# Modulation sums paired with fixed VectorE operations, and the one-row Fourier split ahead of the others

## The chip, the cores and the metric

The kernel runs on one core of a Trainium2 chip. The metric is the device time of one execution in microseconds (us); lower is better.

## What is computed

One layer of a diffusion block on 1024 latent tokens of 1024 features, with 256 context tokens. The reference, cut to what matters here:

```python
mod = cond @ w_mod[l] + b_mod[l]                  # cond = silu(c): one row of 1024
sh1, sc1, g1, sh2, sc2, g2 = jnp.split(mod[:, None, :], N_MOD, axis=-1)
hx = modulate(rmsnorm(x, norm1_g[l]), sh1, sc1)
u_f, u_x, u_g = split(hx @ w_in)                  # 512 features each
y_f = fft2(u_f by groups, norm="ortho").real      # Fourier half, 4 groups of 128
y_r = bidir_rglru(u_x, ...)                       # conv, gates, scans in two directions
x_mix = concat([y_f, y_r * gelu(u_g)]) @ w_out
x = x + g1 * x_mix
hx2 = modulate(rmsnorm(x, norm2_g[l]), sh2, sc2)
x = x + g2 * expert_choice_ffn(hx2, ...)          # 16 experts, top-k routed
return rmsnorm(x, final_g)
```

`sh1` and `sc1` are wanted at once, `g1`, `sh2`, `sc2` and `g2` only after the output projection. Each of these four rows is a sum over 1024 condition values times rows of `w_mod`.

## The kernel before

The program has five parts in time. A prologue (to about 88 us) sums `sh1` and `sc1` on TensorE, norms and transposes the tokens, and projects the first two `u_x` column tiles. `phase_c` (about 88 to 255 us) has the rest of the combined input projection and all that hangs on it. `phase_f` (to about 345 us) has the Fourier matmuls `pq`, the output projection `mx`, the residual and the router. Then a stream of 16 experts (`gu`, `y`) runs to the end, bound by TensorE.

Matmuls are done at full fp32 precision by three products: each operand is split into a high and a low half. ScalarE writes the high half (L227), VectorE the low half as a difference (L228). In names, `wh`/`wl` are the halves of a projection weight (`wr` raw), `gh`/`gl` those of a gate weight, `abh`/`abl` and `xh`/`xl` those of the first Fourier step's result (`ab`, and `abx`, which is a single row). `split` gives one ScalarE and one VectorE instruction; here all splits of `get` and `fb_split` are made at a raised priority.

`phase_c` runs over four tiles t of 128 recurrent features. For each: a projection `ux`, a causal convolution on VectorE (`conv`, L658, result `xc`), gate matmuls `g`, `lru_front` (sigmoids, `r` and `g`; `g*xc` on VectorE, L697 to L700; exponentials to `a` on ScalarE, L707), `lru_back` (a square root on ScalarE, L805, then for each direction the three VectorE operations of `lru_scan`: L713, L714 and the scan L716, and the add of both directions, L813), and `gelu` (projection `ug` of column tile 8+t, a gelu on ScalarE, L821, and a product on VectorE, L822). Beside it run the four Fourier column tiles: `fourier_a` (projection `uf`, VectorE writes sum and difference `U`), then `fb_dft` (`ab`, `abx`), `fb_split`, `fb_trig` (`pq`, a single buffer in PSUM) and `fb_evac` (VectorE operations on `T` and `yf`, L947 to L956, which empty `pq`). `get(ct)` loads and splits the weights of column tile ct: 0 to 3 are `uf`, 4 to 7 `ux`, 8 to 11 `ug`.

The four late modulation rows are summed on VectorE by `mod_acc(r, h)`, called eight times (four rows r, two halves h of 512 columns). One call goes over eight blocks of 128 condition values in four pairs. A pair is one load of 512 KB (`mraw`, two buffers, issued by GpSimd) and two VectorE operations of 128x512 that add it into `macc`; the first of a sum is a TENSOR_SCALAR (L837), the other seven are SCALAR_TENSOR_TENSOR (L839). In all there are 32 loads and 64 operations; the eight sums are stored by GpSimd and read in `phase_f`.

The order of each engine's instructions is set by a tile scheduler when the program is built, by priority (earlier code first, raised for those under `high_priority`) and by when its own model finds operands ready. Instructions handed to `pin` keep their written order among themselves on one engine and are passed through the scheduler as a fixed list; the rest stay free to move. `mod_acc` is not pinned before.

Of the kernel before, what the change touches and what calls it, by code (L numbers as in the profile page):

```python
# [9 lines left out]
F32 = mybir.dt.float32  # L10
# [4 lines left out]
ALU = mybir.AluOpType  # L15

D = 1024
N = 1024
NCTX = 256
L = N + NCTX  # L20
KD = 8
# [140 lines left out]
class Kern:  # L162
# [486 lines left out]
    def conv(self, t):  # L649
        nc = self.nc  # L650
        u = self.u.pop(t)
        xc = self.c5(f"xc{t}", tag="xc")
        col = lambda i: self.cols[:, COL["cw"] + 4 * i + t:COL["cw"] + 4 * i + t + 1]
        cb = self.cols[:, COL["cb"] + t:COL["cb"] + t + 1]
        for o, n, q in ((0, N, NCTX), (N, NCTX, 0)):
            nc.scalar.activation(xc[:, q:q + n], u[:, o:o + n], AF.Identity, scale=col(1), bias=cb)
            for i, a, b in ((0, 1, n), (2, 0, n - 1), (3, 0, n - 2)):
                nc.vector.scalar_tensor_tensor(xc[:, q + a:q + b], u[:, o + a + i - 1:o + b + i - 1], col(i),  # L658
                                               xc[:, q + a:q + b], op0=ALU.mult, op1=ALU.add)
        self.xc[t] = xc  # L660

    def xsplit(self, t):
# [47 lines left out]

    def lru_scan(self, d, r, g, a):
        V = self.nc.vector
        V.scalar_tensor_tensor(r, a, 1.0, r, op0=ALU.add, op1=ALU.mult)  # L713
        V.tensor_tensor(r, r, g, op=ALU.mult)  # L714
        s = slice(None) if d == 0 else slice(None, None, -1)
        V.tensor_tensor_scan(g[:, s], a[:, s], r[:, s], 0.0, op0=ALU.mult, op1=ALU.add)  # L716

    def phase_c(self, stop=None):
        nc = self.nc
        self.xc, self.xs, self.graw, self.gw = {}, {}, {}, {}  # L720
        self.ysp = self.dram.tile([7, 128, N], F32, name="ysp")
        self.yl = {}
        self.accd = self.dram.tile([4, 2, 128, 512], F32, name="accd")
        st = {}
        self.load_gate(0)
        self.conv(0)
        self.xsplit(0)
        self.load_trig()
        self.ux(2)
        self.gate_w(0)  # L730
        self.get(7)
        st[0] = self.lru_front(0)
        self.load_gate(1)
        self.conv(1)
        self.xsplit(1)
        self.ux(3)
        self.get(0)
        self.gate_w(1)
        self.lru_back(0, *st[0])
        self.fourier_a(0)  # L740
        self.mod_acc(0, 0)
        self.conv(2)
        self.get(8)
        self.load_gate(2)
        st[1] = self.lru_front(1)
        self.mod_acc(0, 1)
        self.xsplit(2)
        self.gelu(0)
        self.mod_acc(1, 0)
        self.gate_w(2)  # L750
        self.get(1)
        self.lru_back(1, *st[1])
        self.conv(3)
        self.fourier_a(1)
        self.mod_acc(1, 1)
        self.get(9)
        self.load_gate(3)
        st[2] = self.lru_front(2)
        self.mod_acc(2, 0)
        self.xsplit(3)  # L760
        self.gelu(1)
        self.mod_acc(2, 1)
        self.gate_w(3)
        self.get(2)
        self.lru_back(2, *st[2])
        self.fourier_a(2)
        self.mod_acc(3, 0)
        self.get(3)
        st[3] = self.lru_front(3)
        self.fourier_a(3)  # L770
        self.get(10)
        self.lru_back(3, *st[3])
        self.gelu(2)
        self.get(11)
        self.fd = {}
        self.fb_dft(0)
        self.fb_split(0)
        self.gelu(3)
        self.mod_acc(3, 1)
        if stop == "e":  # L780
            self.fd = {}
            for g in range(CT):
                self.fb_dft(g)
                self.fb_split(g)
                self.fb_trig(g)
                self.fb_evac(g)
# [21 lines left out]
    def lru_back(self, t, st, a):  # L808
        nc = self.nc
        for d in range(2):  # L810
            self.lru_scan(d, *st[d], a[d])
        g0, g1 = st[0][1], st[1][1]
        nc.vector.tensor_tensor(g0[:, NCTX:], g0[:, NCTX:], g1[:, 0:N], op=ALU.add)  # L813
        self.yl[t] = g0[:, NCTX:]

    def gelu(self, t):
        nc = self.nc
        p = self.p2(f"ug{t}")
        self.proj(p, 8 + t)
        gg = self.pr.tile([128, N], F32, tag="gg", name=f"gg{t}", bufs=1)  # L820
        nc.scalar.activation(gg, p, AF.Gelu_apprx_tanh)  # L821
        nc.vector.tensor_tensor(gg, gg, self.yl.pop(t), op=ALU.mult)  # L822
        self.dump(f"yr{t}", gg)
        nc.sync.dma_start(self.ysp[3 + t], gg)

    def mod_acc(self, r, h):
        nc, a = self.nc, self.a
        m, s = (2, 4, 3, 5)[r], slice(512 * h, 512 * h + 512)
        acc = self.pr.tile([128, 512], F32, tag="ht", name=f"macc{m}{h}", bufs=2)
        for kp in range(KD // 2):  # L830
            w = self.pro.tile([128, 2, 512], F32, tag="mraw", name=f"mraw{m}{h}{kp}", bufs=2)
            nc.gpsimd.dma_start(w, a["wmod"][m, 2 * kp:2 * kp + 2, :, s].rearrange("k p c -> p k c"))
            for i in range(2):
                k = 2 * kp + i
                c = self.cond[:, k:k + 1]
                if k == 0:
                    nc.vector.tensor_scalar(acc, w[:, i], c, None, op0=ALU.mult)  # L837
                else:
                    nc.vector.scalar_tensor_tensor(acc, w[:, i], c, acc, op0=ALU.mult, op1=ALU.add)  # L839
        nc.gpsimd.dma_start(self.accd[r, h], acc)  # L840

    def mod_row(self, r, acc, b, ones, p):
        nc = self.nc
# [32 lines left out]
    def fourier_a(self, g):  # L876
        nc = self.nc
        V = nc.vector
        p = self.p2(f"uf{g}")
        self.proj(p, g)  # L880
        U = self.c4(f"U{g}", (128, 2, 512))
        uT = self.pr.tile([128, 512], F32, tag="uT", name=f"uT{g}", bufs=1)
        nc.scalar.activation(uT, p[:, 1023:511:-1], AF.Copy)
        rev = uT[:, 0:511]
        V.tensor_tensor(U[:, 0, 1:], p[:, 1:512], rev, op=ALU.add)
        V.tensor_tensor(U[:, 1, 1:], p[:, 1:512], rev, op=ALU.subtract)
# [19 lines left out]
    def fb_split(self, g):  # L906
        p, px = self.fd[g]
        hi, lo = self.c4(f"abh{g}", (128, 8, 128), F32R), self.c4(f"abl{g}", (128, 8, 128), F32R)
        xh = self.pr.tile([1, 128], F32R, tag="xh", name=f"xh{g}", bufs=1)
        xl = self.pr.tile([1, 128], F32R, tag="xl", name=f"xl{g}", bufs=1)  # L910
        with self.tc.high_priority(offset=self.HP):
            for s in range(2):
                self.split(p[:, 512 * s:512 * s + 512].rearrange("p (a b) -> p a b", b=128),
                           hi[:, 4 * s:4 * s + 4], lo[:, 4 * s:4 * s + 4])
            self.split(px[0:1, 0:128], xh, xl)
        self.fd[g] = hi, lo, xh, xl

    def fb_trig(self, g):
# [910 lines left out]
```

## Time and profile before

| what | us |
|---|---|
| time before, median of 3 runs | 1969.02 (1968.03 to 1969.90) |
| the profiled execution, its own time | 1968.55 |
| its span from first to last instruction | 1966.7 |
| TensorE busy in the span | 1883.7 (96%) |
| VectorE busy | 1749.7 (89%) |
| ScalarE busy | 1357.4 (69%) |
| the 56 SCALAR_TENSOR_TENSOR of `macc` | 41.8 |

All rows below are of one profiled execution. TensorE's matmul stream is PE, its weight loads PEld; VectorE is DVE, ScalarE ACT, GpSimd POOL. A group row gives the busy time and mean duration; an arrow `<-` in square brackets names what ended the idle time ahead of an instruction.

### The profile page before, as it was taken

Reading aid. Unit: us, or ns where it says so; the run is one execution under the profiler, and the core shown is the slowest. Engines: PE = TensorE matmul, PEld = TensorE weight load, DVE = VectorE, ACT = ScalarE, POOL = GpSimd, SP = SyncE. Lnnn points to the kernel's source line nnn. Section 1 sums busy time; section 2 is a strip of 40 time slices with the busy share of each in tenths; the row PEclk is TensorE's granted clock in tenths of the full one; section 3 lists DMA queues with packets and bytes.
Section 4 is the critical chain, followed back from the end, with each engine's and each line's share of the span. In section 5 each row is a group of like instructions: output and inputs, shape, how many; then the busy total and the mean of one; then the engine's idle time right before and its main releaser. Section 6 shows DMA issues by size and latency. Waiting matters only on the chain.

```text
span 1966.7 us, 23514 instructions
## 1 busy us (share of the span) xinstructions
PE 1883.7 (96%) x8944; PEld 1530.9 (78%) x8944; DVE 1749.7 (89%) x1626; ACT 1357.4 (69%) x1094; POOL 126.6 (6%) x126
## 2 busy tenths in 40 slices
PE   7989879969999999999999999999999999999996
PEld 2777767857788888888888888888888888888884
DVE  7889787789999989899999999998989898989987
ACT  6568643346677777777777777777777777777775
POOL 2311100220000000000000000000000000000000
PEclk9999989979999999999999999999999999999998
DMA  8443554578999999999999999999999999999994
GB/s 333 126 148 123 193 174 150 200 279 332 352 352 388 383 376 390 370 395 371 391 362 395 359 409 370 387 364 397 372 384 380 391 379 373 390 383 390 371 391 172
DMA packets 113952, 651.27 MB, mean 331 GB/s; under 512 B 12743, under 2 KB 20472, under 8 KB 46254
## 3 DMA queue, kind: packets, MB, share of 16 engines
q1 hardware_dynamic: 100718, 602.55, 79.6%
q0 software_dynamic: 10816, 38.82, 7.0%
q10 hardware_dynamic: 2304, 8.39, 1.1%
q8 instruction: 70, 1.15, 0.2%
q14 instruction: 44, 0.36, 0.0%
HBM read 622.98 MB, written 26.74 MB: 330 GB/s over the span
## 4 chain that ended last, share of the span: by engine, by line
PE 79%; DVE 8%; DMA 6%; issue 5%; ACT 1%; POOL 0%; SPq 0%; POOLq 0%; DVEq 0%; ACTq 0%
PE gu L611 46%; PE y L611 23%; PE mx L611 4%; DMA mraw<-in_wmod_dram 3%; DVE lo L228 3%; PE ht L1620 2%; DMA wm<-in_wmod_dram 1%; DVE macc L839 1%; PE xt L1492 1%; DMA trr<-in_trig_dram 1%; PE hp L1185 1%; PE pq L611 1%; ACT hi L227 1%; DVE g L716 0%; DVE r L714 0%
## 5 line engine op out<-in xcount | busy, mean ns | idle before, releaser
L228 DVE TENSOR_TENSOR lo<-raw,hi 128x2048 fp32r<-128x2048 f32 x525 | 1196.9, 2295 | 120.6 <-ACT hi L227 119.7
L227 ACT ACTIVATE hi<-raw 128x2048 fp32r<-128x2048 f32 x525 | 1007.0, 1918 | 303.2 <-PE gu L611 204.4
L611 PE MATMUL gu<-hi,xgh 128*128 128x512 f32 x1408 | 556.2, 395 | 0.0
L611 PE MATMUL gu<-lo,xgh 128*128 128x512 f32 x1408 | 548.7, 390 | 1.4 <-DVE lo L228 1.4
L611 PE MATMUL gu<-hi,xgl 128*128 128x512 f32 x1408 | 548.9, 390 | 0.0
L611 PEld LDWEIGHTS gu<-hi,xgl 128*128 128x128 f32 x1408 | 264.4, 188 | 56.4 <-DVE xgl L228 0.2
L611 PEld LDWEIGHTS gu<-lo,xgh 128*128 128x128 f32 x1408 | 264.8, 188 | 55.7 <-DVE lo L228 1.8
L611 PEld LDWEIGHTS gu<-hi,xgh 128*128 128x128 f32 x1408 | 264.6, 188 | 52.7 <-issue 0.2
L611 PE MATMUL y<-hi,hh 128*128 128x512 f32 x704 | 282.0, 401 | 0.0
L611 PE MATMUL y<-hi,hl 128*128 128x512 f32 x704 | 275.9, 392 | 1.3 <-DVE hl L228 1.3
L611 PE MATMUL y<-lo,hh 128*128 128x512 f32 x704 | 274.8, 390 | 0.0
L611 PEld LDWEIGHTS y<-hi,hl 128*128 128x128 f32 x704 | 132.4, 188 | 30.4 <-DVE hl L228 1.8
L611 PEld LDWEIGHTS y<-lo,hh 128*128 128x128 f32 x704 | 132.9, 189 | 25.9 <-issue 0.2
L611 PEld LDWEIGHTS y<-hi,hh 128*128 128x128 f32 x704 | 132.7, 189 | 25.3 <-issue 0.2
L1613 ACT ACTIVATE hid<-gu 128x512 f32<-128x512 f32 x96 | 54.0, 563 | 82.4 <-PE gu L611 82.4
L1630 POOL DMA_INDIRECT accx<-ys,idx x15 | 23.9, 1590 | 1002.8 <-DVE ys L1629 929.7
L228 DVE TENSOR_TENSOR hl<-ht,hh 128x512 fp32r<-128x512 f32 x96 | 61.3, 638 | 0.0
L1614 DVE TENSOR_TENSOR hid<-hid,gu 128x512 f32<-128x512 f32 x96 | 61.0, 635 | 0.0
L839 DVE SCALAR_TENSOR_TENSOR macc<-mraw,cond,macc 128x512 f32<-128x512 f32 x56 | 41.8, 747 | 20.4 <-DMA mraw<-in_wmod_dram 19.5
L1620 PE MATMUL ht<-k_ident,hid 128*128 128x128 f32 x352 | 54.2, 272 | 3.0 <-DVE hid L1614 3.0
L1620 PEld LDWEIGHTS ht<-k_ident,hid 128*128 128x128 f32 x352 | 43.8, 140 | 16.5 <-DVE hid L1614 4.5
L227 ACT ACTIVATE hh<-ht 128x512 fp32r<-128x512 f32 x96 | 52.0, 541 | 1.5 <-PE ht L1620 1.5
(430 smaller groups left out, 1791.4 us busy)
## 6 DMA issues: line engine op xcount, KB each, us to landing
raw<-in_wg_dram SPq DMA_DIRECT2D x160, 1024.0 KB, 7.1
raw<-in_wu_dram SPq DMA_DIRECT2D x160, 1024.0 KB, 7.5
raw<-in_wd_dram SPq DMA_DIRECT2D x160, 1024.0 KB, 7.6
raw<-in_wt_dram SPq DMA_DIRECT2D x32, 1024.0 KB, 7.8
mraw<-in_wmod_dram POOLq DMA_DIRECT2D x32, 512.0 KB, 4.7
raw<-in_wdt_dram SPq DMA_DIRECT2D x16, 1024.0 KB, 6.9
wm<-in_wmod_dram SPq DMA_DIRECT2D x16, 512.0 KB, 9.8
wr<-in_win_dram SPq DMA_DIRECT2D x24, 256.0 KB, 3.6
```

Of the source, the lines that this page charges most:

```text
L227: i = self.nc.scalar.activation(hi, src, AF.Copy)
L228: j = (eng or self.nc.vector).tensor_tensor(lo, src, hi, op=ALU.subtract)
L611: i = nc.tensor.matmul(out, l, r, start=st, stop=sp)
L839: nc.vector.scalar_tensor_tensor(acc, w[:, i], c, acc, op0=ALU.mult, op1=ALU.add)
L1185: self.pin(nc.tensor.matmul(q[:, 1024:1024 + E], hT[:, k], wr[:, k], start=k == 0, stop=k == KD - 1))
L1492: nc.tensor.transpose(p[:, 128 * i:128 * i + 128], xg[:, 128 * k:128 * k + 128], self.ident)
L1613: nc.scalar.activation(hid[:, 0:w], p[:, 0, 0:w], AF.Silu)
L1614: nc.vector.tensor_tensor(hid[:, 0:w], hid[:, 0:w], up, op=ALU.mult)
L1620: self.nc.tensor.transpose(q[:, c:c + 128], hid[:, c:c + 128], self.ident)
L1630: self.nc.gpsimd.indirect_dma_start(out=self.accx, out_offset=bass.IndirectOffsetOnAxis(ap=idx[:, :1], axis=0), in_=ys, in_offset=None, co ...
```

## The change

The eight calls of `mod_acc` are gone. In their place a generator, `mod_gen`, goes through the 32 pairs in order. It issues the load of one pair ahead, and pins loads, sums and stores. `tick(instruction, cost)` stands behind VectorE operations of the convolution, the scans, the add, the gelu product and `fourier_a`, each with a cost in us written in the code, and advances the generator by one pair for each 1.7 us of cost (`STEP`). The operations given to `tick` aren't pinned. Counting starts ahead of the first `lru_back`; pairs that are left are written at the end of `phase_c`. In `fb_split` the one-row split stands first and at doubled priority.

```diff
@@ conv
-                nc.vector.scalar_tensor_tensor(xc[:, q + a:q + b], ...)
+                self.tick(nc.vector.scalar_tensor_tensor(xc[:, q + a:q + b], ...),
+                          1.3 if n == N else 0.5)
@@ lru_scan
-        V.scalar_tensor_tensor(r, a, 1.0, r, op0=ALU.add, op1=ALU.mult)
-        V.tensor_tensor(r, r, g, op=ALU.mult)
+        self.tick(V.scalar_tensor_tensor(r, a, 1.0, r, op0=ALU.add, op1=ALU.mult), 1.5)
+        self.tick(V.tensor_tensor(r, r, g, op=ALU.mult), 1.5)
...
+        self.tick(V.tensor_tensor_scan(g[:, s], a[:, s], r[:, s], 0.0, op0=ALU.mult, op1=ALU.add), 2.8)
@@ phase_c
+        self.mg, self.cost = self.mod_gen(), None
...
         self.gate_w(1)
+        self.cost = 0.0
         self.lru_back(0, *st[0])
         self.fourier_a(0)
-        self.mod_acc(0, 0)
         self.conv(2)
...
-        self.mod_acc(3, 1)
+        for _ in self.mg:
+            pass
@@ lru_back: the add, cost 1.2; gelu: the product, cost 1.2; fourier_a: both U operations, 0.7 each
@@ in place of mod_acc
+    STEP = 1.7
+    def tick(self, i, cost):
+        if self.cost is None:
+            return
+        self.cost += cost
+        while self.cost >= self.STEP:
+            self.cost -= self.STEP
+            next(self.mg, None)
+    def mod_gen(self):
+        nc, a = self.nc, self.a
+        todo = [(r, h, kp) for r in range(4) for h in range(2) for kp in range(KD // 2)]
+        w, acc = {}, {}
+        def load(n):
+            if n < len(todo):
...
+                self.pin(nc.gpsimd.dma_start(w[n], ...))
+        load(0)
+        for n, (r, h, kp) in enumerate(todo):
+            load(n + 1)
...
+                if k == 0:
+                    self.pin(nc.vector.tensor_scalar(acc, w[n][:, i], c, None, op0=ALU.mult))
+                else:
+                    self.pin(nc.vector.scalar_tensor_tensor(acc, w[n][:, i], c, acc, op0=ALU.mult, op1=ALU.add))
+            del w[n]
+            if kp == KD // 2 - 1:
+                self.pin(nc.gpsimd.dma_start(self.accd[r, h], acc))
+            yield
@@ fb_split
         with self.tc.high_priority(offset=self.HP):
+            with self.tc.high_priority(offset=self.HP):
+                self.split(px[0:1, 0:128], xh, xl)
             for s in range(2):
                 self.split(p[:, 512 * s:512 * s + 512].rearrange("p (a b) -> p a b", b=128),
                            hi[:, 4 * s:4 * s + 4], lo[:, 4 * s:4 * s + 4])
-            self.split(px[0:1, 0:128], xh, xl)
```

**First order excerpt.** VectorE at the first pair of scans (`lru_scan` of tile 0, about 127 to 142 us in the trace of before). A number behind a name tells buffers of one tag apart. Before:

```order
L839 SCALAR_TENSOR_TENSOR macc_1369<-mraw_1382,cond,macc_1369 128x512 x2
L837 TENSOR_SCALAR macc_1475<-mraw_1476,cond 128x512
L839 SCALAR_TENSOR_TENSOR macc_1475<-mraw_1476,cond,macc_1475 128x512
L713 SCALAR_TENSOR_TENSOR r_983<-a_1014,r_983 128x1280
L713 SCALAR_TENSOR_TENSOR r_1008<-a_1017,r_1008 128x1280
L228 TENSOR_TENSOR gl_1128<-gr_1022,gh_1127 128x512
L714 TENSOR_TENSOR r_983<-r_983,g_984 128x1280
L714 TENSOR_TENSOR r_1008<-r_1008,g_1009 128x1280
L716 SCALAR_TENSOR_TENSOR g_984<-a_1014,r_983 128x1280
L716 SCALAR_TENSOR_TENSOR g_1009<-a_1017,r_1008 128x1280
L228 TENSOR_TENSOR wl_0_1226<-wr_0_1221,wh_0_1225 128x512
```

And with the change; the lines of the file are shifted, so that L714, L715, L717 and L810 are what L713, L714, L716 and L813 were, and L854 and L856 what L837 and L839 were:

```order
L717 SCALAR_TENSOR_TENSOR g_984<-a_1014,r_983 128x1280
L856 SCALAR_TENSOR_TENSOR macc_1137<-mraw_1133,cond,macc_1137 128x512
L715 TENSOR_TENSOR r_1008<-r_1008,g_1009 128x1280
L856 SCALAR_TENSOR_TENSOR macc_1137<-mraw_1135,cond,macc_1137 128x512
L717 SCALAR_TENSOR_TENSOR g_1009<-a_1017,r_1008 128x1280
L856 SCALAR_TENSOR_TENSOR macc_1137<-mraw_1135,cond,macc_1137 128x512
L810 TENSOR_TENSOR g_984<-g_984,g_1009 128x1024
L856 SCALAR_TENSOR_TENSOR macc_1137<-mraw_1141,cond,macc_1137 128x512
L228 TENSOR_TENSOR wl_0_1259<-wr_0_1254,wh_0_1258 128x512
L856 SCALAR_TENSOR_TENSOR macc_1137<-mraw_1141,cond,macc_1137 128x512
L228 TENSOR_TENSOR wl_1_1263<-wr_1_1256,wh_1_1262 128x512
L856 SCALAR_TENSOR_TENSOR macc_1137<-mraw_1145,cond,macc_1137 128x512
```

Before, 26 modulation operations stand ahead of the first L713 and none between it and the add. With the change none stands ahead of it, and from the scans on they stand between the other operations, two to a pair. From the first L713 (L714 now) to the first `wl` of column tile 10 there are 24 of them before and 54 with the change.

**Second order excerpt.** VectorE at the Fourier splits of group 1 (`xl_2136`, `abl_2134`; `T_2144` and `yf_2145` are the operations that empty `pq` of the group before it). Before:

```order
L228 TENSOR_TENSOR abl_2134<-ab_2089,abh_2133 128x512
L813 TENSOR_TENSOR g_1789<-g_1789,g_1814 128x1024
L228 TENSOR_TENSOR abl_2134<-ab_2089,abh_2133 128x512
L822 TENSOR_TENSOR gg_2037<-gg_2037,g_1789 128x1024
L947 TENSOR_TENSOR T_2144<-pq_2106,T_2143 128x256
L948 TENSOR_TENSOR T_2144<-pq_2106,T_2143 128x256
L949 TENSOR_TENSOR T_2144<-pq_2106,T_2143 128x256
L228 TENSOR_TENSOR xl_2136<-abx_2098,xh_2135 1x128
L950 TENSOR_TENSOR T_2144<-T_2143,pq_2106 128x256
L951 TENSOR_TENSOR yf_2145<-pq_2106,T_2143 128x1
L952 TENSOR_TENSOR yf_2145<-pq_2106,T_2143 128x1
```

With the change:

```order
L870 TENSOR_TENSOR accg_2454<-accg_2454,browg_2456 1x512
L870 TENSOR_TENSOR accg_2455<-accg_2455,browg_2457 1x512
L819 TENSOR_TENSOR gg_2055<-gg_2055,g_1807 128x1024
L228 TENSOR_TENSOR xl_2136<-abx_2098,xh_2135 1x128
L228 TENSOR_TENSOR abl_2134<-ab_2089,abh_2133 128x512 x2
L968 TENSOR_TENSOR T_2144<-pq_2106,T_2143 128x256
L969 TENSOR_TENSOR T_2144<-pq_2106,T_2143 128x256
L970 TENSOR_TENSOR T_2144<-pq_2106,T_2143 128x256
L971 TENSOR_TENSOR T_2144<-T_2143,pq_2106 128x256
```

The one-row split stood behind both 512-wide splits and three of the `T` operations; now it stands ahead of all of them.

**Third order excerpt.** ScalarE at the gelu of the third `ug` projection (`gg_1951` before, `gg_1969` now) and the exponential of the last scan's second direction (`a_1822` before, `a_1840` now). Before:

```order
L821 ACT_TABLE_LOAD
L821 ACTIVATE gg_1951<-ug_1902 128x1024
L227 ACTIVATE xh_1980<-abx_1976 1x128
L227 ACTIVATE woh_2188<-wor_2083 128x512
L707 ACT_TABLE_LOAD
L707 ACTIVATE a_1822<-r_1813,cneg 128x1280
L227 ACTIVATE abh_1978<-ab_1967 128x512
```

With the change:

```order
L708 ACT_TABLE_LOAD
L708 ACTIVATE a_1840<-r_1831,cneg 128x1280
L818 ACT_TABLE_LOAD
L818 ACTIVATE gg_1969<-ug_1920 128x1024
L709 ACTIVATE r_1831<-r_1831,chalf 128x1280
L227 ACTIVATE xh_1998<-abx_1994 1x128
```

The exponential and its table load stood behind the gelu and stand ahead of it now.

## Rows read from the trace of the kernel before

**Rows 1.** Waits of TensorE, 100 to 320 us: total, times, longest, us.
```profile
PE ug L611 <- DVE wl L228: 8.6, 2, 6.8
PE abx L903 <- DVE xl L228: 6.4, 1, 6.4
PE uf L611 <- DVE wl L228: 5.4, 1, 5.4
PE pq L611 <- DVE abl L228: 2.1, 1, 2.1
```

**Rows 2.** Stretches by engine: us, busy of PE, PEld, DVE, ACT, POOL, then PEclk, DMA, GB/s.
```profile
88.00:128.70 40.70, 40.70 (x208) 34.50 (x207) 30.09 (x39) 26.29 (x29) 9.50 (x14) 1.00 0.57 175
128.70:224.50 95.80, 81.56 (x353) 65.31 (x352) 86.28 (x95) 64.17 (x61) 10.16 (x15) 0.95 0.40 127
250.50:282.00 31.50, 21.16 (x132) 18.53 (x133) 28.53 (x54) 13.93 (x24) 0.58 (x1) 0.84 0.57 192
```

**Rows 3.** The first stretch, instructions on `macc` alone: busy of DVE and POOL.
```profile
88.00:128.70 40.70, 17.69 (x24) 1.70 (x3) 1.00 0.57 175
```

**Rows 4.** Waits of VectorE, 128.7 to 224.5 us.
```profile
DVE macc L839 <- DMA mraw<-in_wmod_dram: 5.9, 3, 4.0
```

**Rows 5.** Loads of `mraw`: issue ns min/median/max with first and last start, and landing.
```profile
L832 POOL DMA_DIRECT2D mraw<-in_wmod_dram x32: 704/712/742, 72.9 to 246.8; - x32
...
DMA to landing us min/median/max: 4.1/4.7/7.8
```

**Rows 6.** Timeline of VectorE and GpSimd: start, us, engine, line, operation.
```profile
81.02 0.75 DVE L839 SCALAR_TENSOR_TENSOR macc<-mraw,cond,macc 128x512 f32<-128x512 f32 x1
...
82.08 0.70 POOL L832 DMA_DIRECT2D mraw<-in_wmod_dram  x1 [7.06 <-DVE macc L839]
...
128.70 2.89 DVE L713 SCALAR_TENSOR_TENSOR r<-a,r 128x1280 f32<-128x1280 f32 x2
...
140.94 1.22 DVE L813 TENSOR_TENSOR g<-g,g 128x1024 f32<-128x1024 f32 x1
...
223.81 0.74 DVE L839 SCALAR_TENSOR_TENSOR macc<-mraw,cond,macc 128x512 f32<-128x512 f32 x1
224.47 0.68 DVE L228 TENSOR_TENSOR wl<-wr,wh 128x512 fp32r<-128x512 f32 x1
...
250.45 0.27 DVE L228 TENSOR_TENSOR xl<-abx,xh 1x128 fp32r<-1x128 f32 x1
...
268.02 0.27 DVE L228 TENSOR_TENSOR xl<-abx,xh 1x128 fp32r<-1x128 f32 x1
```

**Rows 7.** Timeline of ScalarE.
```profile
123.17 2.44 ACT L805 ACTIVATE r<-r 128x1280 f32<-128x1280 f32 x2
...
249.27 1.36 ACT L707 ACTIVATE a<-r,cneg 128x1280 f32<-128x1280 f32 x1 [3.54 <-DVE g L716]
...
257.39 1.28 ACT L821 ACT_TABLE_LOAD   x1
258.69 1.02 ACT L821 ACTIVATE gg<-ug 128x1024 f32<-128x1024 f32 x1
```

**Rows 8.** Timeline of TensorE.
```profile
226.59 0.39 PE L611 MATMUL ug<-hTh,wl 128*128 128x512 f32 x1
...
237.03 2.04 PE L900 MATMUL ab<-dft,U 128*128 128x128 f32 x16
...
239.30 0.50 PE L611 MATMUL ug<-hTh,wh 128*128 128x512 f32 x1
...
250.53 1.68 PE L900 MATMUL ab<-dft,U 128*128 128x128 f32 x12
...
275.20 2.08 PE L900 MATMUL ab<-dft,U 128*128 128x128 f32 x16
...
278.42 0.48 PE L611 MATMUL pq<-trig,abh 128*128 128x258 f32 x2 [0.83 <-DVE yf L952]
...
282.01 0.40 PE L611 MATMUL mx<-woh,yth 128*128 128x512 f32 x1
```

More of the change, by code (lines that the diff above doesn't have):

```diff
@@ L657, in conv @@
             for i, a, b in ((0, 1, n), (2, 0, n - 1), (3, 0, n - 2)):
-                nc.vector.scalar_tensor_tensor(xc[:, q + a:q + b], u[:, o + a + i - 1:o + b + i - 1], col(i),
-                                               xc[:, q + a:q + b], op0=ALU.mult, op1=ALU.add)
+                self.tick(nc.vector.scalar_tensor_tensor(xc[:, q + a:q + b], u[:, o + a + i - 1:o + b + i - 1],
+                                                         col(i), xc[:, q + a:q + b], op0=ALU.mult, op1=ALU.add),
+                          1.3 if n == N else 0.5)
         self.xc[t] = xc
@@ L712, in lru_scan @@
         V = self.nc.vector
-        V.scalar_tensor_tensor(r, a, 1.0, r, op0=ALU.add, op1=ALU.mult)
-        V.tensor_tensor(r, r, g, op=ALU.mult)
+        self.tick(V.scalar_tensor_tensor(r, a, 1.0, r, op0=ALU.add, op1=ALU.mult), 1.5)
+        self.tick(V.tensor_tensor(r, r, g, op=ALU.mult), 1.5)
         s = slice(None) if d == 0 else slice(None, None, -1)
-        V.tensor_tensor_scan(g[:, s], a[:, s], r[:, s], 0.0, op0=ALU.mult, op1=ALU.add)
+        self.tick(V.tensor_tensor_scan(g[:, s], a[:, s], r[:, s], 0.0, op0=ALU.mult, op1=ALU.add), 2.8)
     def phase_c(self, stop=None):
@@ L745, in phase_c @@
         st[1] = self.lru_front(1)
-        self.mod_acc(0, 1)
         self.xsplit(2)
         self.gelu(0)
-        self.mod_acc(1, 0)
         self.gate_w(2)
@@ L754, in phase_c @@
         self.fourier_a(1)
-        self.mod_acc(1, 1)
         self.get(9)
@@ L758, in phase_c @@
         st[2] = self.lru_front(2)
-        self.mod_acc(2, 0)
         self.xsplit(3)
         self.gelu(1)
-        self.mod_acc(2, 1)
         self.gate_w(3)
@@ L766, in phase_c @@
         self.fourier_a(2)
-        self.mod_acc(3, 0)
         self.get(3)
@@ L812, in lru_back @@
         g0, g1 = st[0][1], st[1][1]
-        nc.vector.tensor_tensor(g0[:, NCTX:], g0[:, NCTX:], g1[:, 0:N], op=ALU.add)
+        self.tick(nc.vector.tensor_tensor(g0[:, NCTX:], g0[:, NCTX:], g1[:, 0:N], op=ALU.add), 1.2)
         self.yl[t] = g0[:, NCTX:]
@@ L821, in gelu @@
         nc.scalar.activation(gg, p, AF.Gelu_apprx_tanh)
-        nc.vector.tensor_tensor(gg, gg, self.yl.pop(t), op=ALU.mult)
+        self.tick(nc.vector.tensor_tensor(gg, gg, self.yl.pop(t), op=ALU.mult), 1.2)
         self.dump(f"yr{t}", gg)
         nc.sync.dma_start(self.ysp[3 + t], gg)
-    def mod_acc(self, r, h):
-        nc, a = self.nc, self.a
[L828 to L832, printed above, removed]
+    STEP = 1.7
[7 more added lines that the diff above has]
+    def mod_gen(self):
+        nc, a = self.nc, self.a
+        todo = [(r, h, kp) for r in range(4) for h in range(2) for kp in range(KD // 2)]
+        w, acc = {}, {}
+        def load(n):
+            if n < len(todo):
+                r, h, kp = todo[n]
+                m, s = (2, 4, 3, 5)[r], slice(512 * h, 512 * h + 512)
+                w[n] = self.pro.tile([128, 2, 512], F32, tag="mraw", name=f"mraw{m}{h}{kp}", bufs=2)
+                self.pin(nc.gpsimd.dma_start(w[n], a["wmod"][m, 2 * kp:2 * kp + 2, :, s].rearrange("k p c -> p k c")))
+        load(0)
+        for n, (r, h, kp) in enumerate(todo):
+            load(n + 1)
+            if kp == 0:
+                acc = self.pr.tile([128, 512], F32, tag="ht", name=f"macc{r}{h}", bufs=2)
             for i in range(2):
@@ L836, in mod_acc @@
                 if k == 0:
-                    nc.vector.tensor_scalar(acc, w[:, i], c, None, op0=ALU.mult)
+                    self.pin(nc.vector.tensor_scalar(acc, w[n][:, i], c, None, op0=ALU.mult))
                 else:
-                    nc.vector.scalar_tensor_tensor(acc, w[:, i], c, acc, op0=ALU.mult, op1=ALU.add)
-        nc.gpsimd.dma_start(self.accd[r, h], acc)
+                    self.pin(nc.vector.scalar_tensor_tensor(acc, w[n][:, i], c, acc, op0=ALU.mult, op1=ALU.add))
[3 more added lines that the diff above has]
+            yield
     def mod_row(self, r, acc, b, ones, p):
@@ L884, in fourier_a @@
         rev = uT[:, 0:511]
-        V.tensor_tensor(U[:, 0, 1:], p[:, 1:512], rev, op=ALU.add)
-        V.tensor_tensor(U[:, 1, 1:], p[:, 1:512], rev, op=ALU.subtract)
+        self.tick(V.tensor_tensor(U[:, 0, 1:], p[:, 1:512], rev, op=ALU.add), 0.7)
+        self.tick(V.tensor_tensor(U[:, 1, 1:], p[:, 1:512], rev, op=ALU.subtract), 0.7)
         V.tensor_copy(U[:, 0, 0:1], p[:, 0:1])
```

## Prediction

> **What bounds the kernel now.** I read the waits of TensorE first, because it is busy for nearly the whole span and only its gaps can be won. Between 100 and 320 us they are few, and VectorE ends the longest: 8.6 us at `ug` and 5.4 us at `uf` for the low half of a weight split (`wl`), 6.4 us at `abx` for the one-row split `xl`, 2.1 us at `pq` for `abl` [rows 1]. Next the stretches by engine [rows 2]. From 88 to 128.7 us TensorE is busy 40.70 of 40.70 us and VectorE 30.09: VectorE has slack there and holds nobody up. From 128.7 to 224.5 us VectorE is busy 86.28 of 95.8 us and TensorE 81.56. There VectorE is the engine that the others wait for, so what counts is when its list ends, not how TensorE's list looks. Of its 9.5 idle us there, 5.9 are waits of the running sums for loads of modulation weights [rows 4]. From 250.5 to 282 us TensorE is busy 21.16 of 31.5 us at a mean clock of 0.84; at the lower of its two levels (1.2 against 2.4 GHz) that is a third of the time. After 282 us the two kernels have the same work on TensorE in the same order, so the forecast is the shift of one event: the first `mx` matmul, 282.01 us before [rows 8].
>
> **What the change takes away and puts back on VectorE.** The 64 modulation operations stay; only their place changes. In the stretch with slack, 24 of them took 17.69 us [rows 3]; two more stand just ahead of it. The changed order has none before the first scan product. There VectorE would sit idle instead, since that product waits for ScalarE's square root: the pair of roots runs from 123.17 us for 2.44 us, so the first is there at about 124.4 [rows 7]. The first product then starts at 124.5 in place of 128.70 [rows 6]: 4.2 us won. TensorE wins nothing here, because it had no gap.
>
> Now the list from there to the split that TensorE needs for the third gelu projection: the first `wl` of column tile 10, which starts at 224.47 us [rows 6]. The changed order holds 54 modulation operations in that stretch where 24 stood: 26 came from ahead of it and 4 from behind. Beside other work one costs 0.66 us (223.81 to 224.47, [rows 6]), so 30 add 19.8 us. The `g*xc` product of the last scan pair for the second direction also moves ahead of the split, an estimated 1.5 us by the 1.2 us of the add of the same length [rows 6]. Work: 86.3 + 19.8 + 1.5 = 107.6 us. From 124.5 us, with no idle time, that ends at **232.1 us**, 7.6 us later than before. This is the core of the forecast: work leaves a stretch where it was covered and enters one where it is not.
>
> **Waits for loads.** Two buffers hold the weights, so a pair's load goes out only when the pair two before it is done. The operation that ends at 81.77 us is followed by the issue at 82.08 [rows 6], 0.3 us, and the load lands 4.1 us after its issue at least, 4.7 in the median, 7.8 at most [rows 5]. Where less than some 5.1 us of VectorE work stands between the end of one pair and the start of the next but one, VectorE waits, in order, with scans and weight splits queued behind. An example is the first order excerpt: between the last operation on `mraw_1135` and the first on `mraw_1145` stand one add (1.2 us, [rows 6]), two modulation operations (1.3) and two splits (0.68 alone [rows 6], an estimated 0.6 each where operations overlap as 0.74 becomes 0.66), 3.7 us in all, so 1.4 us is lost. I went through the 27 pairs of the stretch in this way, counting each operation at its distance to the next one: at a landing time of 4.7 us 11 places lose 10.1 us, at 4.2 us 8 places lose 5.3, at 5.0 us 11 lose 13.1, at 5.5 us 12 lose 18.6. I take the median, since loads that follow each other by 1.5 to 4 us are the rule in both orders. What else was idle before, 3.6 us (9.5 - 5.9), I set to zero: it would fall into these waits. The split then starts at **X = 242.2 us** (232.1 + 10.1).
>
> The Trainium skill, "DMA: Bandwidth & Descriptors", section "Anatomy of one DMA — SWDGE (gpsimd) path", fits 2.0 us plus the bytes by 436 GB/s; an estimate for these 512 KB by it is 3.2 us, and by it no place would lose anything and X would be 232. The rows say 4.1 at the least, so the sum goes by them.
>
> **TensorE from X on.** Up to X its gaps only mirror VectorE's list (its four gate groups now stand closer together, so it also waits for ScalarE, but its 81.56 us of work in that stretch stand against 113.5 us now, 128.7 to X). From X it runs: the rest of the third `ug` 10.4 us (226.59 to 237.03), `ab` and `abx` 2.3 (to 239.30), the fourth `ug` 11.2 (to 250.53), `ab`/`abx` 2.3, and then `pq` 3.6 (278.42 to 282.01) three times with 3.2 us between (275.20 to 278.42), in which `ab` and `abx` run and VectorE empties the single `pq` buffer [rows 8]. One new wait comes in. On ScalarE an exponential now stands ahead of the gelu that frees the buffer of the fourth `ug` (third order excerpt), and it waits for the scan that ends about 10.6 us after X. Exponential 1.36, table load 1.28, gelu 1.02 [rows 7]: free at X + 14.4, while TensorE is there at X + 12.7: 1.7 us lost. Sum: 10.4 + 2.3 + 1.7 + 11.2 + 2.3 + 3.6 + 3.2 + 3.6 + 3.2 + 3.6 = 45.1 us. `mx` would start at 242.2 + 45.1 = 287.3 us, against 282.01: **5.3 us later**.
>
> What is won back lies in this tail. Before, `mx` comes 55.4 us after 226.59; here 45.1 us after X. With all modulation sums out of the way, the one-row split of group 1 starts about 13.5 us after that of group 0 (TensorE's own pace, 11.2 + 2.3) in place of 17.6 (250.45 to 268.02, [rows 6]), and the 6.4 us gap and the low clock behind it go. The bound on the clock: if it falls all the same, the middle `pq` takes up to 3.6 us more.
>
> **The one-row split put first** I cost at nothing. For group 0 it already stood ahead of the other two in VectorE's order. For group 1 it moves ahead of two splits (second order excerpt), but `pq` of that group also needs the single buffer that the last group's `T` and `yf` operations empty; for the last group the trace names `yf` as what `pq` waits for [rows 8], and half of those operations stood behind `xl` before. So moving `xl` alone brings `pq` no sooner. Were the buffer free in time, it could win up to 1.2 us (two splits of 0.6); were the two splits what `pq` waits for last, it could lose 0.2 us, `xl`'s own length [rows 6].
>
> **The rivals.**
> 1. *Level.* Loads land after 4.2 to 4.5 us, as lone loads do (4.1 is the least). At 4.2, X is 237.4, and `mx` comes 0.5 us late: 1969.0 us. For it: an even spacing of 3 to 4 us, not bursts. Against it: the median of before holds such spacings too. Chance 0.30.
> 2. *Faster.* The loads are always in time because each was sent a pair ahead, so X is 232.1 and `mx` starts 4.8 us early, or 6.5 without the gelu's wait: 1962 to 1964 us. It decides at a landing time below about 3.7 us (then 1.6 us is lost). For it: most of VectorE's waits before lay in bursts. Against it: no load of the trace was that quick. Chance 0.17. The skill's figure above would lead here.
> 3. *Slower by more.* Near 230 us the loads meet SyncE's reads of weights in HBM; the longest landing, 7.8 us, is that of such a meeting, I take it. At 5.5 us throughout, X is 250.7 and `mx` 13.8 us late: 1982.4 us, with the clock's 3.6 us 1986. Chance 0.13. A rule of the skill speaks for it ("SBUF — State Buffer", section "SBUF: two separate sides"): certain VectorE operations lock GpSimd out of a shared port, so it can't write descriptors. By it, loads issued in a stretch where VectorE never rests would land later. The 32 issues took 704 to 742 ns each [rows 5], so no row here shows it.
> 4. *The change doesn't do what it says.* If pairs had stayed in bursts, the order would show them; it shows them apart, so this has no chance of its own.
>
> **How the numbers follow.** The profiled execution took 1968.55 us with a span of 1966.7; the median of the runs is 1969.02, 0.5 us more. Forecast: 1968.55 + 5.3 = 1973.9 by the profiled execution; with a little of the 0.5 us, 1974.0. Its chance is 0.40. The range reaches from rival 2's upper end with a part of it left out, 1964.5, to rival 3's lower part, 1982; about 0.2 lies outside. A measurement of this kernel can tell about 0.2%, 3.9 us, from no change. Slower by more than that holds most of the forecast and all of rival 3: 0.50. Within it: rival 1 and the forecast's lower edge, 0.33. Faster: rival 2, 0.17.
>
> **What would show each step.** VectorE's waits for `mraw` between 125 and 240 us: about 10 us, in some eleven places of about 1 us (right), under 3 us (rival 2), over 15 (rival 3). VectorE idle from about 118 to 124.5 us. The `wl` of column tile 10 near 242 us. No gap at `abx` of 6 us, a short one at the fourth `ug` with ScalarE's gelu as releaser, and a full clock from 250 us on. The forecast is wrong if TensorE reaches `mx` before 282 us, or if a gap after 282 us that is in neither order decides.

## The result and the profile after

The changed kernel took 1983.22 us (median of 5 runs, 1980.79 to 1987.17) against 1969.02 for the kernel before: a ratio of 1.0066, 95% interval 1.0054 to 1.0079. By the ratio it is 13 us slower, by the two medians 14.2. The direction was forecast, the size was not: 1974.0 had been predicted and the range ended at 1982.0. The profiled execution took 1983.22 us, with a span of 1981.4.

The stretches of the profile after, by engine, with the columns of [rows 2]: from 88 us to the first scan product (126.41 us), to the third gelu projection (246.17 us), to the first `mx`.

```profile
88.00:126.40 38.40, 38.40 (x198) 32.56 (x197) 14.87 (x19) 22.54 (x23) 0.00 (x0) 1.00 0.11 35
126.40:246.20 119.80, 94.24 (x381) 74.61 (x379) 106.72 (x126) 73.48 (x71) 21.80 (x32) 0.91 0.53 163
246.20:296.50 50.30, 44.75 (x247) 37.65 (x247) 41.95 (x69) 25.05 (x35) 3.97 (x6) 0.93 0.66 224
```

The same three stretches, modulation operations (`macc`) alone: busy time of VectorE and GpSimd.

```profile
88.00:126.40 38.40, 0.00 (x0) 0.00 (x0) 1.00 0.11 35
126.40:246.20 119.80, 38.36 (x54) 3.38 (x6) 0.91 0.53 163
246.20:296.50 50.30, 7.21 (x10) 1.14 (x2) 0.93 0.66 224
```

The first stretch holds none of the 24 operations of [rows 3], and VectorE is busy there for 14.87 us where it was for 30.09. The second holds 54. It is 119.8 us long where 128.70 to 226.13, the same two events, took 97.4 before.

What VectorE waited for in that stretch: total, times, longest, us.

```profile
DVE macc L856 <- DMA mraw<-in_wmod_dram: 7.5, 6, 2.1
DVE r L714 <- ACT r L802: 7.3, 1, 7.3
DVE macc L854 <- DMA mraw<-in_wmod_dram: 5.5, 5, 2.6
```

Eleven waits for loads, 13.0 us together, answer to [rows 4]. Beside that row the trace of before has one more wait of this kind in its stretch, so that 13.0 stand against 7.1:

```profile
DVE macc L837 <- DMA mraw<-in_wmod_dram: 1.2, 1, 1.2
```

The 7.3 us is the slack ahead of the first scan product, which stands empty now. The timeline of VectorE at that product, and of TensorE at the events of [rows 8]:

```profile
126.41 2.89 DVE L714 SCALAR_TENSOR_TENSOR r<-a,r 128x1280 f32<-128x1280 f32 x2 [7.29 <-ACT r L802]
```

```profile
257.38 2.04 PE L920 MATMUL ab<-dft,U 128*128 128x128 f32 x16
...
263.53 0.79 PE L611 MATMUL ug<-hTh,wh 128*128 128x512 f32 x1 [3.80 <-ACT gg L818]
...
277.03 2.04 PE L920 MATMUL ab<-dft,U 128*128 128x128 f32 x16
...
296.50 0.40 PE L611 MATMUL mx<-woh,yth 128*128 128x512 f32 x1
```

The first `mx` starts at 296.50 us, 14.5 later than before. From there to the end of the span both need the same: 1966.7 - 282.0 = 1684.7 us before and 1981.4 - 296.5 = 1684.9 after.

One thing must be kept apart. Up to about 70 us the two kernels do the same, yet the first `ux` matmul of `phase_c` starts at 85.63 us in the profile of before and at 87.53 in that of after; in the fifteen profiles of this study it lies between 85.6 and 90.0 us. So 1.9 of the 14.5 us belong to these two executions, not to the change. Below, times inside the program are therefore counted from the first `ux` or between two events: from `ux` to `mx` it is 196.4 us before and 209.0 after.

### The profile page after: what moved, and what is told of

It reads as the page before. It is cut to its first block, busy times and chain, and to the rows that moved or that the text cites. A ratio compares the mean times of both kernels' runs of the same rounds, so it can differ in the third digit from the quotient of the medians.

```text
span 1981.4 us, 23517 instructions
## 1 busy us (share of the span) xinstructions
PE 1892.2 (95%) x8944; PEld 1536.4 (78%) x8944; DVE 1746.5 (88%) x1626; ACT 1358.0 (69%) x1093; POOL 125.9 (6%) x126
## 4 chain that ended last, share of the span: by engine, by line
PE 78%; DVE 4%; issue 1%; ACT 1%; DMA 1%; POOLq 0%; DVEq 0%; ACTq 0%
PE gu L611 46%; PE y L611 23%; PE mx L611 4%; DVE lo L228 2%; PE ht L1641 2%; PE xt L1513 1%; PE hp L1206 1%; ACT hi L227 1%; DMA raw<-in_wg_dram 1%; DMA xg<-hxd,idx 0%; PE pq L611 0%; PE hp L1197 0%; ACT junkf L1686 0%; PE mx7a L611 0%; PE mx7b L611 0%
## 5 line engine op out<-in xcount | busy, mean ns | idle before, releaser
L856 DVE SCALAR_TENSOR_TENSOR macc<-mraw,cond,macc 128x512 f32<-128x512 f32 x56 | 41.8, 746 | 12.8 <-DMA mraw<-in_wmod_dram 12.7
```

The source lines that it names most:

```text
L856: self.pin(nc.vector.scalar_tensor_tensor(acc, w[n][:, i], c, acc, op0=ALU.mult, op1=ALU.add))
```

## The experiments

**The two parts of the change apart.** The changed kernel with the old `fb_split` (run e1; the others are numbered in the same way):

```diff
-            with self.tc.high_priority(offset=self.HP):
-                self.split(px[0:1, 0:128], xh, xl)
             for s in range(2):
                 self.split(p[:, 512 * s:512 * s + 512]...)
+            self.split(px[0:1, 0:128], xh, xl)
```

> The changed kernel with the old order in fb_split: only the pairs. The modulation operations stand on VectorE as in the changed kernel (none ahead of the first scan product, 54 ahead of the first wl of column tile 10, 64 ahead of the first xl). Theory (the pairs cost all of it): 1981 to 1986 us, the same as the changed kernel within 2 us. Rival (the one-row split put first costs a good part, by delaying the wide splits that pq waits for): 1972 to 1979 us.

It took 1983.25 us, ratio to the kernel before 1.0054 (1.0037 to 1.0070). And the kernel before with the new `fb_split` alone (e2, the same diff the other way round):

> The kernel before with only the one-row split put first. Theory: 1967 to 1971 us, no change within 2 us, since pq also needs the buffer that T and yf empty. Rival (the split's place costs): 1974 us or more. A gain of over 3 us (the 6.4 us wait at abx shortened) would speak against both.

It took 1970.40 us, ratio 1.0001 (0.9991 to 1.0010). As far as some 2 us can be told, the pairs are the whole effect and the split is none. The waits of TensorE of this second kernel, 100 to 320 us, show why:

```profile
PE ug L611 <- DVE wl L228: 8.6, 2, 6.8
PE pq L611 <- DVE yf L953: 5.0, 2, 4.6
PE uf L611 <- DVE wl L228: 4.4, 1, 4.4
PE pq L611 <- DVE abl L228: 1.9, 1, 1.9
```

The 6.4 us wait at `abx` of [rows 1] is gone, and a wait of 4.6 us for `yf` at the next `pq` stands in its place: the buffer that `T` and `yf` empty was late next, as the prediction had it.

**Place.** Counting starts at the head of `phase_c` (e3):

```diff
-        self.mg, self.cost = self.mod_gen(), None
+        self.mg, self.cost, self.STEP = self.mod_gen(), 0.0, 0.85
...
-        self.cost = 0.0
+        self.cost, self.STEP = 0.0, 3.8
         self.lru_back(0, *st[0])
```

> The changed kernel with its pairs in other places: counting starts at the head of phase_c with a step of 0.85 us up to the first lru_back, and a step of 3.8 us from there on. 16 modulation operations then stand ahead of the first scan product (0 in the changed kernel, 26 before) and 48 ahead of the first wl of column tile 10 (54 and 50). So that stretch holds 32, against 54 and 24. Theory (what costs is the number of operations in the stretch where VectorE is the bound): 22 fewer by 0.66 us and about half of the 13 us of waits for loads, so 1962 to 1970 us. Rival (pairing itself costs: a pinned row of pairs with waits in the middle of scans): 1977 us or more.

It took 1977.58 us, ratio 1.0035 (1.0024 to 1.0047). That lies in the rival's range, at its lower end. But VectorE's timeline ahead of the first scan product shows another reason than the rival's:

```profile
117.92 0.41 DVE L701 TENSOR_TENSOR g<-g,xc 128x256 f32<-128x256 f32 x1
129.63 1.54 DVE L854 SCALAR_TENSOR_TENSOR macc<-mraw,cond,macc 128x512 f32<-128x512 f32 x2 [11.29 <-DMA mraw<-in_wmod_dram]
131.08 1.49 DVE L714 SCALAR_TENSOR_TENSOR r<-a,r 128x1280 f32<-128x1280 f32 x1
```

GpSimd issues the modulation loads in pinned order with the eight loads and casts of the Fourier tables, which share the two buffers. With pairs written ahead of the tables, those ran from 106.12 to 125.04 us between two pairs' loads. So the tables were moved ahead (e6):

```diff
         self.load_gate(0)
+        self.load_trig()
         self.conv(0)
         self.xsplit(0)
-        self.load_trig()
```

> The early counting of the run e3_early, and the Fourier tables' loads written ahead of the first pairs, since there the pinned order put 18 us of table loads and casts on GpSimd between two pairs' loads, and VectorE stood 11.3 us for a load. 24 operations now stand ahead of the first scan product and 52 ahead of the first wl of column tile 10: the stretch holds 28. Theory (place and waits, the pin itself costs nothing): the 11.3 us wait goes, 1964 to 1970 us. Rival (pinned pairs cost wherever they are): 1975 us or more.

It took 1965.51 us, ratio 0.9971 (0.9961 to 0.9982): the same pinned pairs, 24 of the operations back in the slack, and the kernel is faster than before. So it isn't true that pinned pairs cost wherever they are. `macc` alone in its three stretches (the same events; two of the 24 stand ahead of 88 us):

```profile
88.00:128.80 40.80, 15.83 (x22) 1.15 (x2) 1.00 0.59 186
128.80:226.80 98.00, 19.79 (x29) 2.23 (x4) 0.93 0.44 140
226.80:277.40 50.60, 8.55 (x12) 1.14 (x2) 0.93 0.66 214
```

The middle stretch has 29 operations in 98.0 us, where the changed kernel has 54 in 119.8. In the kernel before it took 97.4 us, so the gain over that kernel isn't there: in the profiles it is in the tail, 50.6 us from the third gelu projection to `mx` against 55.9. How much of it the earlier table loads bring isn't shown, since no run moves them alone. With a step of 5 us in place of 3.8 behind the first `lru_back`, more move on into the tail (e7):

> As e6_early_trig_first with a step of 5 us from the first lru_back on: 24 operations ahead of the first scan product, 22 in the stretch up to the wl of column tile 10, 18 behind it. Theory: by e6's cost per operation the third gelu projection starts some 4 us earlier, but the tail holds 6 operations more, 4 us of VectorE where TensorE waits for the Fourier splits, so within 3 us of e6, 1963 to 1971 us. If the tail had slack it would be 4 us faster than e6.

It took 1972.93 us, ratio 1.0010 (1.0000 to 1.0019), 7 us above the run before it. Both halves of the expectation were too mild: from the first scan product to the third gelu projection it was 92.5 us in place of 98.1, 5.6 us earlier, and from there to `mx` 61.7 in place of 50.6, 11.2 us longer. The tail has no slack either. TensorE's waits in it:

```profile
PE pq L611 <- DVE yf L971: 12.9, 2, 8.8
```

**The pin.** The loads, sums and stores of `mod_gen` without `self.pin`, all else as changed (e5):

```diff
-                    self.pin(nc.vector.scalar_tensor_tensor(acc, w[n][:, i], c, acc, ...))
+                    nc.vector.scalar_tensor_tensor(acc, w[n][:, i], c, acc, ...)
```

> The changed kernel with the modulation loads, sums and stores left free to move; the pairs are written at the same ticks. In the built order 26 operations again stand ahead of the first scan product, as before (0 in the changed kernel), and 54 ahead of the first wl of column tile 10 (54; 50 before), so that stretch holds 28 (54; 24 before). Theory (place decides, and it is the pin that took the operations out of the stretch with slack): 1966 to 1974 us. Rival (what costs is that the pairs stand among the scans and weight splits, wherever they were written): 1978 us or more.

1974.29 us, ratio 1.0018 (1.0008 to 1.0027), 0.3 us above the theory's range: 9 us of the 14 come back. Left free, the scheduler puts 26 operations into the slack again. What is left lies in the stretch behind it: 107.0 us from the first scan product to the third gelu projection, with 38 operations.

**Waits for loads.** The changed kernel with two of its 32 loads (e4):

```diff
+                if n > 1:
+                    w[n] = w2[n % 2]
+                    return
-                w[n] = self.pro.tile(...)
+                w2[n] = w[n] = self.pro.tile(...)
```

> The changed kernel with only the first two of its 32 modulation loads; all 64 VectorE operations stay and read these two buffers, so the sums are of the wrong weights and no operation waits for a load. The scheduler puts some of them elsewhere, but none ahead of the first scan product and 54 to 64 ahead of the weight splits of the third gelu projection. Theory (30 operations of work, plus the waits): the 13 us of waits go, work stays; 1969 to 1975 us. Rival 1 (waits for loads are the whole of it): 1963 us or less. Rival 2 (the waits only fill time in which VectorE would wait for ScalarE or TensorE anyway): 1980 us or more.

And the same done to the kernel before, as its control (e8):

> The kernel before with only its first two modulation loads; the 64 VectorE operations stay, on the wrong weights, and wait for no load. It is the control for e4_two_loads. 37 operations stand ahead of the first scan product and 26 in the stretch up to the wl of column tile 10. Theory (place costs beside the waits): 1958 to 1964 us, below e4 by the work moved, 5 to 12 us. Rival (waits for loads are all of the difference between the two kernels): the same as e4_two_loads within 2 us, 1968 to 1972 us.

The first took 1969.67 us, ratio 0.9994 (0.9984 to 1.0004), inside the theory's range. The second took 1948.76 us, ratio 0.9884 (0.9867 to 0.9901), lower than any theory had it. Without a single wait for a load the two places are still 21 us apart. The stretches between first scan product, third gelu projection and `mx`, first of the changed kernel with two loads:

```profile
126.40:240.20 113.80, 91.95 (x380) 72.73 (x379) 113.80 (x138) 72.59 (x71) 4.37 (x8) 0.91 0.19 62
240.20:284.50 44.30, 41.96 (x247) 35.84 (x247) 33.99 (x57) 25.61 (x35) 0.00 (x0) 1.00 0.55 180
```

and of the kernel before with two loads:

```profile
128.00:216.80 88.80, 83.66 (x371) 67.58 (x369) 87.62 (x96) 68.18 (x68) 1.62 (x3) 0.98 0.18 60
216.80:264.30 47.50, 43.84 (x257) 37.29 (x256) 38.04 (x63) 30.37 (x41) 0.54 (x1) 1.00 0.56 183
```

In the first VectorE is busy for 113.80 of 113.80 us: it never rests in that stretch. It holds 64 modulation operations, the second 26, and 38 by 0.66 us are 25.1 us, against 25.0 us between the two lengths. (The scheduler, which knew of no loads to wait for, put 10 more into the first than the changed kernel has, and 11 more ahead of the second than the kernel before has; so the 21 us are for 38 operations moved, not 30. That 25.1 and 25.0 agree so closely is in part luck: with two loads, the changed kernel's first `wl` of column tile 10 starts at 236.70 us, 3.5 us ahead of the projection. Counted to that split, the two lists are 110.3 and 88.7 us long.)

**Size of a load.** Each pair's load issued as two of 256 KB, in the changed kernel (e9), in the kernel before (e11), and in the kernel with early pairs and tables first (e10):

```diff
-                self.pin(nc.gpsimd.dma_start(w[n], a["wmod"][m, 2 * kp:2 * kp + 2, :, s]...))
+                for i in range(2):
+                    self.pin(nc.gpsimd.dma_start(w[n][:, i], a["wmod"][m, 2 * kp + i, :, s]))
```

> The changed kernel with each load of a pair issued as two loads of 256 KB, one for each operation; places, pin and the two buffers stay (none ahead of the first scan product, 58 ahead of the first wl of column tile 10, where 54 stood). The sum of the prediction lost 10.1 us at a landing of 4.7 us, 5.3 at 4.2 and 1.6 at 3.7. Theory (the waits scale with the landing of each load): the first half lands after about 4 us, waits in the stretch fall from 13 to 5 to 8 us, 1976 to 1980 us. Rival (waits are set by the second half, or by GpSimd's 0.7 us for each issue): no change, 1981 us or more.

> The kernel before with loads of 256 KB: the control for the two runs above. Its bursts leave no work between a pair and the next but one, so that the waits are long. Theory: half a microsecond for each wait that matters, 1964 to 1969 us. Rival (in a burst a load's whole landing counts, and two issues cost more): 1970 us or more.

> e6_early_trig_first with loads of 256 KB. 24 operations ahead of the first scan product and 28 in the stretch, as in e6. Theory: what is left of waits for loads in e6 (11.4 us from 88 to 290 us) falls by half, 1959 to 1964 us. Rival: two issues for each pair make it no faster, 1965 us or more.

They took 1978.56 us (ratio 1.0032, 1.0018 to 1.0046), 1964.12 us (0.9963, 0.9949 to 0.9977) and 1960.88 us (0.9941, 0.9924 to 0.9957): 5 to 7 us less than with whole loads, all inside the theory's range. Loads of the changed kernel, from issue to landing:

```profile
DMA to landing us min/median/max: 4.2/4.8/7.4
```

and of the same with halves:

```profile
DMA to landing us min/median/max: 3.0/4.1/6.2
```

The waits for loads in the bound stretch went from 13.0 to 9.7 us, not to the 5 to 8 of the theory. And waits are at most a part of the gain. In the profiles, first `ux` to first `mx` got shorter by 3.5 us in the changed kernel (209.0 to 205.4), by 2.9 in the kernel before (196.4 to 193.5) and by 0.2 in the early version (190.5 to 190.4). The rest lies behind the first `mx`, where no modulation load runs: there these three kernels need 1684.7 to 1685.0 us with whole loads and 1680.5 to 1681.2 with halves, all of it in the last 25 us. Why it is shorter there stays open. The last of the three is the best version found, 10 us below the kernel before. With a step of 0.7 in place of 0.85, so that 28 operations stand ahead of the first scan product (e12):

> As e10 with a step of 0.7 us up to the first lru_back: 28 operations ahead of the first scan product (24 in e10), 26 in the stretch up to the wl of column tile 10 (28), 10 behind it (12). Theory (what leaves the stretch gains 0.66 us each, as long as it fits in the slack ahead): 1 to 3 us below e10. Rival (the slack ahead is full, since loads come at one pair for some 3.2 us, and 14 pairs need 45 us): the first scan product starts later, and it is 0 to 4 us above e10.

1961.80 us, ratio 0.9943 (0.9926 to 0.9959), not to be told from it. The trace bears the rival out: the first scan product starts 46.9 us after the first `ux` matmul in place of 40.1. The slack ahead is full at about 24.

**The tail.** The term of the prediction that missed by most was the tail, so the order named in it was undone: ScalarE's gelu ahead of the last exponential (e13). `lru_late` holds the exponential, tanh and root of the second direction, which stood in `lru_front`; the gelu and that exponential are pinned.

```diff
+        self.gelu(2)
+        self.lru_late(3, *st[3])
         self.lru_back(3, *st[3])
-        self.gelu(2)
...
+        if t == 2:
+            self.pin(i)
```

> The changed kernel with ScalarE's gelu of the third projection set ahead of the last scan's exponential, which the built order had put ahead of it. VectorE's list up to the third gelu projection and TensorE's order are those of the changed kernel. In the changed kernel TensorE waited 3.8 us for that gelu, and the fourth gelu projection ran 2.3 us longer behind it, at the lower clock. Theory (the tail's miss is this order): both go and the last scan follows some 3 us later than now, so the first mx comes 3 to 6 us earlier, 1977 to 1980 us. Rival (the scan, its square root and the weight splits behind it only take the place of the wait, since pq needs them): mx within 2 us of the changed kernel, 1981 to 1985 us.

1984.94 us, ratio 1.0074 (1.0060 to 1.0088): the rival. TensorE's waits from the third gelu projection to `mx` (the one for `U` stands just ahead of that projection), first of the changed kernel, then of this one:

```profile
PE ug L611 <- ACT gg L818: 3.8, 1, 3.8
PE ug L611 <- DVE U L908: 1.8, 1, 1.8
PE pq L611 <- DVE yf L973: 1.7, 2, 1.5
```

```profile
PE pq L611 <- DVE yf L982: 4.1, 1, 4.1
PE ug L611 <- DVE U L917: 2.3, 1, 2.3
PE ug L611 <- ACT gg L825: 1.0, 1, 1.0
```

The wait for the gelu shrank from 3.8 to 1.0 us, and the one for `yf` grew from 1.7 to 4.1. Low clock came behind that one instead. The first `mx` came 211.9 us after the first `ux`, against 209.0. Of these 2.9 us, 1.4 come from the third projection, which took 12.6 us here against 11.2, at a lower granted clock:

```profile
245.20:257.80 12.60, 12.60 (x49) 10.09 (x50) 9.76 (x12) 5.66 (x8) 2.69 (x4) 0.86 0.86 311
```

Undoing the order on ScalarE alone doesn't shorten the tail.

## Why the prediction was wrong

**What bounds the kernel, right.** Work in the stretch behind the first scan product lengthens it by about its own duration: e6, e5 and the pair e4 and e8 all show it. In the slack ahead the work is free, the waits for its loads are not: with 37 operations there and no waits (e8) the product starts 38.9 us after the first `ux` matmul, as with none; with loads and 24 operations (e6) it is 41.9.

**The slack and the work, right.** The first scan product was to come 4.2 us earlier: it starts 38.9 us after the first `ux` matmul in place of 43.1. VectorE's work in the stretch was to be 107.6 us: 106.72 measured. (One reading was off: of the 9.5 us that VectorE was idle in the stretch before, 7.1 were waits for loads and not 5.9, with the wait at L837 shown above. The sum didn't use it.)

**Waits for loads, right in kind, 2.9 us short.** Eleven places were forecast and eleven are there, with 13.0 us where the sum had 10.1. That is what its own list gave for a landing of 5.0 us; the median landing was 4.8. So X, forecast at 242.2, came at 246.09 us:

```profile
246.09 1.29 DVE L228 TENSOR_TENSOR wl<-wr,wh 128x512 fp32r<-128x512 f32 x2
```

The 3.9 us between are +1.9 of the later prologue, +2.9 of waits and -0.9 of work.

**The tail, the step that failed.** "From X on it runs": 45.1 us were summed from TensorE's own list, at the full clock and with a single wait of 1.7 us for ScalarE. The trace has 50.4. The 5.3 us stand on TensorE's list as 2.1 for the gelu (a wait of 3.8), 2.3 for the fourth `ug` at the lower clock behind it, and 0.9 since the third `ug` waited from its first matmul and not from its first low half. So of the 10.3 us that the tail was to win (55.4 to 45.1), 5.0 came. The scan that the exponential waits for ended 11.0 us after X, where the sum had 10.6. But the exponential began 2.7 us behind it, because it brought its own table load and stood behind a split of an output weight that waited for that weight's load:

```profile
254.29 2.82 DVE L717 TENSOR_TENSOR_SCAN g<-a,r 128x1280 f32<-128x1280 f32 x1
...
257.83 0.63 ACT L227 ACTIVATE woh<-wor 128x512 fp32r<-128x512 f32 x1 [3.96 <-DMA wor<-in_wout_dram]
258.48 1.28 ACT L708 ACT_TABLE_LOAD   x1
259.78 1.36 ACT L708 ACTIVATE a<-r,cneg 128x1280 f32<-128x1280 f32 x1
261.16 1.28 ACT L818 ACT_TABLE_LOAD   x1
262.45 1.02 ACT L818 ACTIVATE gg<-ug 128x1024 f32<-128x1024 f32 x1
```

e13 shows that repairing this term alone brings nothing: with the order undone, VectorE's operations of the last scan start 27.7 us behind the first `wl` in place of 24.9, and `pq` waits for what stands behind them. So a second chain is nearly as late as the gelu. The sum followed VectorE behind X only to the end of one scan; but on its list ten modulation operations are still to come there, with four waits for loads:

```profile
DVE macc L856 <- DMA mraw<-in_wmod_dram: 5.2, 3, 4.1
...
DVE macc L854 <- DMA mraw<-in_wmod_dram: 0.5, 1, 0.5
```

That is 7.2 us of work (the third row of `macc` above) and 5.7 of waits, among the last scan's operations and the Fourier splits. How much of the 5.3 us is theirs no run isolates. Over the profiles, third gelu projection to `mx` took 44.3 and 48.5 us with none of them in it (e4, e5), 46.0 and 48.1 with six (e12, e9), 50.3, 52.3 and 53.1 with ten (the changed kernel, e1, e13) and 61.7 with eighteen (e7). So the tail grows with them; but kernels with the same number are 2 to 4 us apart, and their orders differ elsewhere too (in e4 the fourth projection waits for `U` and not for the gelu). That part of the cause stays open.

**The clock, wrong.** "The low clock behind it goes" did not hold. The gap of 3.8 us is followed by a granted clock at the lower level (1.2 against 2.4 GHz), and the fourth `ug` takes 13.5 us against 11.2 for the third. The two as windows (the clock is the third number from the end):

```profile
246.20:257.40 11.20, 11.20 (x49) 9.03 (x50) 9.88 (x10) 5.00 (x6) 2.69 (x4) 1.00 0.87 295
...
263.50:277.00 13.50, 13.47 (x48) 10.93 (x49) 9.44 (x12) 7.86 (x10) 0.58 (x1) 0.80 0.61 199
```

A bound of 3.6 us for it had been put on the middle `pq`, and into rival 3 only, not beside the forecast. A new gap had been forecast, and the price of the clock behind it belonged to the same term.

**The sum.** 5.3 us forecast, +1.9 prologue, +2.9 loads, -0.9 work, +5.3 tail (from X to `mx`, 246.09 to 296.50, 50.4 against 45.1): 14.5 us, as measured. Without the 1.9 us of the prologue, which are chance, it is 12.6.

**The rivals.** Level and faster fell: loads land no earlier than in the kernel before. The time is that of rival 3, but not by its mechanism. Landing at 5.5 us throughout did not happen. GpSimd's issues took the same 704/712/742 ns while VectorE was fullest, as before. Of the rule of the Trainium skill that VectorE can lock GpSimd out of a shared port ("SBUF — State Buffer", section "SBUF: two separate sides") no run here shows anything. The range ended in rival 3's lower part, 1.2 us short of the measured time: it had no room for two errors in the same direction, in the waits and in the tail.

**The one-row split, right**, in its time (e2) and in what is late next (`yf`).

**What the change did bring.** With loads, the two kernels are about 13 us apart; without any wait for loads 21 us. The 8 us between are not what spacing the pairs saves: 5.3 of them are the eight operations more (38 for 30, by 0.66 us) that the runs without loads move. VectorE's waits for modulation loads fell from 25.4 to 18.7 us between 86 us and `mx`, but 10.1 of the 25.4 lay in the slack. Behind the first scan product they rose from 15.3 to 18.7 us, for 64 operations in place of 38. So spacing made the mean wait for each operation shorter, and moving the operations into the bound stretch cost far more than that.

## What to carry to other kernels

Filler work belongs where the engine that does it has slack, not where it can be spread evenly: count the operations in each stretch between two events that bound the kernel, and see whether a pin has taken away the scheduler's choice to fill a gap with them. When an engine is the bound up to some event, it remains in the sum behind that event until its own list there is shown to be hidden; a sum of the waiting engine's work alone is a lower bound. If filler waits for loads through two buffers, smaller loads are worth trying: here 256 KB in place of 512 KB were 5 to 7 us in three different orders, of which at most 3.5 us lay where the loads are.

## What the runs showed of the hardware

A load of 512 KB in two halves of 256 KB landed 0.7 us earlier in the median (4.8 to 4.1 us), at 536 ns for each issue where a whole one takes 712; both the halves and the wholes went out on GpSimd's queue. The first `ux` matmul started at 85.63 us in the profile of before and at 89.65 in that of e2, which has the same instructions ahead of it: 4.0 us, a third of the effect measured here. A profile of before and one of after should be laid over each other at an event behind such a stretch, not at the start.
